# Prompt band attention with the values as matmul weights, two heads in the two column halves of the array

## The chip, the cores and the metric

The kernel runs on one core of a Trainium2 chip. The metric is the device time of one execution in microseconds (us); the median of several runs is reported. Each run of the kernel before is listed below; the profile is that of one further execution.

## What is computed

One step of a one-layer encoder on a prompt of 2048 frames and a sample of 8 x 16 frames: a mixer (band attention beside a convolution), a cross-attention into 256 memory tokens, and a squared-ReLU MLP. The change is in the band attention of the prompt, which has 8 heads of width 64; a frame of chunk c (64 frames) sees the frames of chunks c-8 to c:

```python
s = jnp.einsum('bnqhd,bnkhd->bnhqk', qc, kb).astype(jnp.float32) * (Dh ** -0.5)
s = s + rel_bias(table, q_off, k_off).astype(jnp.float32)[None, None]
s = jnp.where(key_valid[None, :, None, None, :], s, NEG_INF)
p = jax.nn.softmax(s, axis=-1).astype(v.dtype)
o = jnp.einsum('bnhqk,bnkhd->bnqhd', p, vb)
```

## The kernel before, in words

The mixer works through four sets q of four 128-frame tiles (`QT`, line 187; the sample is a fifth tile of set 0). For each set it computes the projections q, k, v and the two GLU halves, writes Q, K and V to scratch in HBM, and runs the convolution as 31 taps on VectorE over four channel blocks (line 451, held in order by a token). The attention of set q runs while set q+1 is projected; that of the last set runs beside the output projection.

The attention of a set (`attn`, line 609) goes head by head, and within a head over its four query tiles i. `attn_load` brings in the head's Q, K, V and bias (lines 537 to 544; K is the tile `ak`, which has two buffers, V is `av`). `scores` multiplies in TensorE (line 564), adds the bias and finds the minimum on VectorE (line 568), and takes the exponential on ScalarE, which also sums it (line 571). `xpose` turns the up to five 128 x 128 blocks of probabilities on TensorE (line 585) and copies them out of PSUM on ScalarE (line 587). `values` multiplies each turned block as the weights (128 columns) with 64 columns of V (line 597) and adds up to five blocks in PSUM (tile `oc`, one buffer). After the fourth tile VectorE takes the reciprocal of the sums (line 602) and scales the result into `a` (line 604); every second head the pair is written to `catd` (line 607). The tiles 0 to 3 of set 0 have 1, 2, 3 and 4 blocks, all the others five: 70 blocks a head, 560 for eight heads.

All pieces are put in one list by times written out by hand (`Plan`, `PAR`, `pl.add(..., attn(q))`, lines 818 to 825); within a stretch the functions of `attn` are spread evenly. That list gives the priority. A scheduler then fixes the order on each engine ahead of the run: of the instructions whose inputs and buffers it reckons ready, the first in the list. So the pieces of one function can be parted by others, and each engine executes its own queue in the order so fixed. Loads of the attention go through SP's queue with those of the weights. All operands of line 597 are F32; the large products of line 122 and the scores are F32R.

Of the kernel before, what the change touches and what calls it, by code (L numbers as in the profile page):

```python
# [11 lines left out]
F32 = mybir.dt.float32  # L12
F32R = mybir.dt.float32r
BF16 = mybir.dt.bfloat16
AF = mybir.ActivationFunctionType
ALU = mybir.AluOpType
# [57 lines left out]
class Kern:  # L74
# [93 lines left out]
    def mixer(self):  # L168
# [4 lines left out]
        with ExitStack() as st:  # L173
# [42 lines left out]
            def bias_tables():  # L216
                anti = mp.tile([P, P], F32, tag="t512", name="anti")
                nc.gpsimd.memset(anti, 0.0)
                nc.gpsimd.affine_select(out=anti, in_=anti, compare_op=ALU.not_equal, fill=1.0,
                                        base=-(P - 1), pattern=[[1, P]], channel_multiplier=1)  # L220
                tab = mp.tile([H, 257], F32, tag="att", name="tab")
                nc.sync.dma_start(tab, I["att_rel_bias"][0])
                ext = mp.tile([H, 768], F32, tag="ak", name="ext")
                nc.vector.tensor_copy(ext[:, 0:256], tab[:, 1:257])
                nc.vector.tensor_copy(ext[:, 256:768], tab[:, 256:257].to_broadcast([H, 512]))
                nc.sync.dma_start(extd, ext)
                far = mp.tile([P, H], F32, tag="far", name="far", bufs=1)
                nc.sync.dma_start(far, view(I["att_rel_bias"], 256, [[0, P], [257, H]]))
                z = mp.tile([P, 384], F32, tag="apr", name="zero")
                nc.gpsimd.memset(z, 0.0)  # L230
                for h in range(H):
                    hk = mp.tile([P, 2, P], F32, tag="av", name="hk")
                    for m in range(2):
                        nc.sync.dma_start(hk[:, m, :], view(extd, h * 768 + m * P, [[1, P], [1, P]]))
                    pt = ps.tile([P, 512], F32, tag="tp", name="pt", bufs=TPB)
                    for m in range(2):
                        nc.tensor.matmul(pt[:, (1 - m) * P:(2 - m) * P], hk[:, m, :], anti, start=True, stop=True)
                    bt = mp.tile([P, 640], F32, tag="ab", name="bt")
                    nc.vector.tensor_scalar(bt[:, 0:384], z, far[:, h:h + 1], -1.0, op0=ALU.add, op1=ALU.mult)
                    nc.vector.tensor_scalar(bt[:, 384:640], pt[:, 0:256], -1.0, None, op0=ALU.mult)  # L240
                    nc.gpsimd.memset(bt[64:128, 0:64], BIG)
                    nc.gpsimd.memset(bt[0:64, 576:640], BIG)
                    nc.sync.dma_start(biasd[h], bt)
                hs = mp.tile([P, 2, P], F32, tag="av", name="hs")
                nc.sync.dma_start(hs[:, 0, :].rearrange("p (h q) -> p h q", h=H), view(extd, P, [[1, P], [768, H], [1, 16]]))
                nc.sync.dma_start(hs[:16, 1, :].rearrange("p (h q) -> p h q", h=H), view(extd, 112, [[1, 16], [768, H], [1, 16]]))
                pt = ps.tile([P, 512], F32, tag="tp", name="pt", bufs=TPB)
                nc.tensor.matmul(pt[:, 0:P], hs[:, 0, :], anti, start=True, stop=True)
                nc.tensor.matmul(pt[:, P:P + 16], hs[:16, 1, :], anti[:16, P - 16:], start=True, stop=True)
                nc.vector.tensor_scalar(sbias[:, 0:P], pt[:, 0:P], -1.0, None, op0=ALU.mult)  # L250
                nc.gpsimd.memset(sbias[:, P:480], BIG)
                nc.vector.tensor_scalar(sbias[:, 240:256], pt[:, P:P + 16], -1.0, None, op0=ALU.mult)
# [273 lines left out]
                return fns  # L526


            A, KQ, PEND, READY = {}, {}, [], []

            def attn_load(q, h):
                def fn():
                    t0 = QT[q][0]
                    k0 = max(0, t0 - 4)
                    nk = t0 + 4 - k0
                    qt = mp.tile([P, 512], F32R, tag="aq", name="aq")
                    nc.sync.dma_start(fr(qt), Qd[h].rearrange("a d t -> (a d) t")[:, t0 * P:t0 * P + 512])
                    kt = mp.tile([P, 2, 1024], F32R, tag="ak", name="ak")
                    for j in range(2):
                        nc.sync.dma_start(fr(kt)[j * HD:(j + 1) * HD, :, :nk * P], Kd[h, :, :, k0 * P:(k0 + nk) * P].rearrange("a d t -> d a t"))  # L540
                    vt = mp.tile([P, 8, HD], F32, tag="av", name="av")
                    nc.sync.dma_start(vt[:, :nk, :], Vd[k0 * P:(k0 + nk) * P, h].rearrange("(j p) d -> p j d", p=P))
                    bt = mp.tile([P, 640], F32, tag="ab", name="ab")
                    nc.sync.dma_start(bt, biasd[h])
                    ss = mp.tile([P, 4], F32, tag="ass", name="ass")
                    KQ[q, h] = (qt, kt, vt, bt, ss, k0)
                return fn

            def scores(q, h, i):
                def fn():  # L550
# [17 lines left out]
                    nc.vector.tensor_tensor_reduce(v3(tt[:, :n]), sp[:, :nb, :w], v3(bt[:, 640 - n:]), op0=ALU.add, op1=ALU.min,  # L568
                                                   scale=1.0, scalar=3e38, accum_out=mn)
                    pr = mp.tile([P, 640], F32, tag="apr", name="apr")  # L570
                    nc.scalar.activation(pr[:, :n], tt[:, :n], AF.Exp, bias=mn, scale=-1.0, accum_out=ss[:, i:i + 1])
                    PEND.append((q, h, i, pr, n, j0 - k0))
                return fn

# [2 lines left out]
            def xpose():  # L577
                q, h, i, pr, n, jo = PEND.pop(0)
                nj = n // P
                pt = mp.tile([P, 5, P], F32, tag="apt", name="apt")  # L580
                for a, b in ((0, min(nj, 3)), (3, nj)):
                    if a < b:
                        tp = ps.tile([P, 512], F32, tag="tp", name="tpa", bufs=TPB)[:, :(b - a) * P]
                        for j in range(a, b):
                            nc.tensor.transpose(tp[:, (j - a) * P:(j - a + 1) * P], pr[:, j * P:(j + 1) * P], self.ident)
                        dst, src = pt[:, a:b, :], tp.rearrange("p (j q) -> p j q", j=b - a)
                        nc.scalar.activation(dst, src, AF.Copy)
                READY.append((q, h, i, pt, nj, jo))

            def values():  # L590
                q, h, i, pt, nj, jo = READY.pop(0)
                qt, kt, vt, bt, ss, k0 = KQ[q, h]
                if i == 0:
                    OC[q, h] = ps.tile([P, 4, HD], F32, tag="oc", name="oc")
                oc = OC[q, h]
                for j in range(nj):
                    nc.tensor.matmul(oc[:, i, :], pt[:, j, :], vt[:, jo + j, :], start=j == 0, stop=j == nj - 1)
                if i == 3:
                    if h % 2 == 0:
                        A[q] = mp.tile([P, 4, P], F32, tag="a", name="a")  # L600
                    r = mp.tile([P, 4], F32, tag="ar", name="ar")
                    nc.vector.reciprocal(r, ss)
                    c = (h % 2) * HD
                    nc.vector.tensor_tensor(A[q][:, :, c:c + HD], oc, r.unsqueeze(2).to_broadcast([P, 4, HD]), op=ALU.mult)
                    if h % 2:
                        t0 = QT[q][0]
                        nc.sync.dma_start(catd[t0 * P:(t0 + 4) * P, (h - 1) * HD:(h + 1) * HD].rearrange("(i p) c -> p i c", p=P), A[q])

            def attn(q):
                fns = [attn_load(q, 0)]  # L610
                for n in range(4 * H + 2):
                    h, i = n // 4, n % 4
                    if n < 4 * H:
                        fns.append(scores(q, h, i))
                    if 0 < n <= 4 * H:
                        fns.append(xpose)
                    if n > 1:
                        fns.append(values)
                    if i == 2 and h + 1 < H:
                        fns.append(attn_load(q, h + 1))  # L620
                return fns


# [7 lines left out]
            def sattn_load(b):  # L631
                def fn():
# [3 lines left out]
                    cv = mp.tile([P, DA], F32, tag="sv", name="scv")  # L636
                    nc.sync.dma_start(cv, I["cache_attn_v"][0, b].rearrange("t h d -> t (h d)"))
                    K = mp.tile([P, 4, 2, 256], F32R, tag="ak", name="sk")
                    Q = mp.tile([P, 4, 2, P], F32R, tag="sqb", name="sq")
                    qs = mp.tile([P, 4, 2, 16], F32, tag="a", name="qs")  # L640

                    nc.gpsimd.memset(fr(Q), 0.0)
# [35 lines left out]
            def sattn_values(b):  # L678
                def fn():
                    V, pr = SA.pop(b)  # L680
                    tp = ps.tile([P, 512], F32, tag="tp", name="tps", bufs=TPB)
                    for s in range(2):
                        nc.tensor.transpose(tp[:, s * P:(s + 1) * P], pr[:, s * P:(s + 1) * P], self.ident)
                    PT = mp.tile([P, 2, P], F32, tag="apt", name="spt")
                    nc.scalar.activation(PT.rearrange("p s c -> p (s c)"), tp[:, :256], AF.Copy)
                    ov = ps.tile([P, 4, 32], F32, tag="oc", name="ov")
                    for p in range(4):
# [726 lines left out]
```

## Time and profile before

| | us |
|---|---|
| runs of the kernel before | 3266.02, 3258.2, 3266.6 (median 3266.02) |
| the profiled execution | 3256.27 |
| its span | 3254.5 |
| TensorE busy | 3129.9 (96%) |
| TensorE weight loads busy | 2679.6 (82%) |
| VectorE busy | 1827.2 (56%) |
| ScalarE busy | 1234.0 (38%) |

A busy time is a sum over instructions that may overlap on the pipelined TensorE; how long a run of matmuls takes is better read from where it begins to where the next one begins. Every F32 matmul leaves two records of a weight load and two of a matmul: line 597 issues 560 and shows 1120. The prompt attention lies between 318 and 1010 us: set 0 from 318, set 1 from 454, set 2 from 692, set 3 from 857 us. The last convolution tap ends at 827 us, the output projection begins after 880 us.

### The profile page before, as it was taken

How to read it: one execution, taken by the hardware profiler on the slowest of the kernel's cores; microseconds unless marked ns; L12 is line 12 of the kernel's file. 1: busy time of each engine (PE TensorE's matmuls, PEld its weight loads, DVE VectorE, ACT ScalarE, POOL GpSimd, SP SyncE). 2: the span in 40 equal slices, each digit the busy share in tenths (PEclk: the TensorE clock that was granted, in tenths of full speed). 3: DMA queues.
4: the chain of work that ended last, by engine and by line, in shares of the span. 5: the costliest groups of instructions: out<-in, count | busy, mean ns of one | idle time of the engine just before them, and what ended most of it. 6: DMA issues, size and time to landing. Idle time of an engine off the chain costs nothing. (4 is left out here: it accounts for less than half of the span.)

```text
span 3254.5 us, 44695 instructions
## 1 busy us (share of the span) xinstructions
PE 3129.9 (96%) x16664; PEld 2679.6 (82%) x16664; DVE 1827.2 (56%) x2812; ACT 1234.0 (38%) x2499; POOL 614.6 (19%) x704
## 2 busy tenths in 40 slices
PE   8889999999899999999999999999999999999998
PEld 7787788979898768788888999988888888888887
DVE  6798979788634435433335444455445544465444
ACT  3223454534554435422224232333334333343332
POOL 4346253342313320022221000002000200020000
PEclk9999999999899999999999999999999999999999
DMA  5465766747864565322224222234233432243222
GB/s 188 122 175 159 210 171 166 195 122 193 241 176 160 189 202 180 102 65 66 64 86 148 81 75 81 75 107 151 93 104 118 145 104 95 91 142 123 91 94 75
DMA packets 309352, 425.18 MB, mean 131 GB/s; under 512 B 62984, under 2 KB 177680, under 8 KB 309062
## 3 DMA queue, kind: packets, MB, share of 16 engines
q1 hardware_dynamic: 300574, 391.38, 40.5%
q0 software_dynamic: 8560, 30.94, 2.4%
q8 instruction: 131, 2.15, 0.3%
q14 instruction: 87, 0.71, 0.1%
HBM read 356.60 MB, written 69.52 MB: 131 GB/s over the span
## 5 line engine op out<-in xcount | busy, mean ns | idle before, releaser
L122 PE MATMUL pu<-xT,wu 128*128 128x512 f32 (+1 forms) x3840 | 756.3, 358 | 3.2 <-DVE xT L95 2.5
L122 PE MATMUL pd<-wd,h 128*128 128x512 f32 x3264 | 750.6, 390 | 1.4 <-DVE y L1336 1.1
L122 PEld LDWEIGHTS pu<-xT,wu 128*128 128x128 f32 x3840 | 659.9, 188 | 95.8 <-DVE xT L95 2.7
L122 PEld LDWEIGHTS pd<-wd,h 128*128 128x128 f32 x3264 | 611.3, 188 | 129.8 <-DVE y L1336 1.5
L122 PE MATMUL pm<-xT,w 128*128 128x512 f32 (+3 forms) x1992 | 423.2, 363 | 11.8 <-POOL w L95 6.2
L451 DVE SCALAR_TENSOR_TENSOR acc<-u,wdT,acc 128x512 f32<-128x512 f32 x480 | 429.7, 895 | 6.4
L103 POOL TENSOR_SCALAR nm<-nss 128x1 f32<-128x1 f32 x103 | 29.7, 288 | 2025.8 <-ACT nsq L132 1078.6
L122 PEld LDWEIGHTS pm<-xT,w 128*128 128x128 f32 x1992 | 337.6, 194 | 52.0 <-POOL w L95 6.5
L94 ACT ACTIVATE wd<-wst 128x512 fp32r<-128x512 f32 x256 | 159.8, 631 | 430.9 <-PE pd L122 364.5
L95 POOL TENSOR_TENSOR w<-wst,w 128x512 fp32r<-128x512 f32 x154 | 229.1, 1502 | 319.9 <-ACT w L94 296.2
L1336 DVE TENSOR_TENSOR y<-pd,y 128x512 f32<-128x512 f32 x238 | 163.5, 688 | 205.0 <-PE pd L122 204.9
L1318 DVE SCALAR_TENSOR_TENSOR hh<-pu,r 128x512 f32<-128x512 f32 (+1 forms) x160 | 96.8, 609 | 321.1 <-ACT r L1317 320.9
L1317 ACT ACTIVATE r<-pu 128x512 f32<-128x512 f32 (+1 forms) x160 | 83.8, 528 | 364.6 <-PE pu L122 356.5
L95 DVE TENSOR_TENSOR wu<-wst,wu 128x512 fp32r<-128x512 f32 x256 | 170.9, 690 | 86.7 <-ACT wu L94 85.7
L95 DVE TENSOR_TENSOR wd<-wst,wd 128x512 fp32r<-128x512 f32 x256 | 182.1, 735 | 35.7 <-ACT wd L94 35.1
L122 PE MATMUL pm<-wo,cT 128*128 128x512 f32 x816 | 200.4, 398 | 0.0
L94 ACT ACTIVATE wu<-wst 128x512 fp32r<-128x512 f32 x256 | 157.7, 630 | 100.6 <-DMA wst<-w_ffn_up 69.2
L122 PE MATMUL y<-mo,pT 128*128 128x512 f32 x768 | 187.1, 398 | 0.0
L122 PE MATMUL sc<-m,xT 128*128 128x512 f32 x768 | 182.0, 392 | 0.3 <-ACT xT L94 0.2
L122 PEld LDWEIGHTS pm<-wo,cT 128*128 128x128 f32 x816 | 151.3, 189 | 33.6 <-issue 2.9
L122 PEld LDWEIGHTS y<-mo,pT 128*128 128x128 f32 x768 | 142.9, 188 | 33.2
L122 PEld LDWEIGHTS sc<-m,xT 128*128 128x128 f32 x768 | 142.9, 188 | 30.8 <-DVE xT L95 0.5
(246 smaller groups left out, 3677.0 us busy)
## 6 DMA issues: line engine op xcount, KB each, us to landing
wst<-w_ffn_up SPq DMA_DIRECT2D x256, 256.0 KB, 3.2
wst<-w_ffn_down SPq DMA_DIRECT2D x256, 256.0 KB, 3.1
wst<-w_in SPq DMA_DIRECT2D x160, 256.0 KB, 3.9
ak<-Kd SPq DMA_DIRECT2D x48, 512.0 KB, 6.8
ab<-biasd SPq DMA_DIRECT2D x32, 320.0 KB, 4.2
cx<-catd SPq DMA_DIRECT2D x17, 512.0 KB, 7.4
x1d<-oy POOLq DMA_DIRECT2D x17, 512.0 KB, 5.9
nx<-x1d SPq DMA_DIRECT2D x17, 512.0 KB, 4.1
```

Of the source, the lines that this page charges most:

```text
L94: nc.scalar.activation(hi, src, AF.Copy)
L95: return (lo_eng or nc.vector).tensor_sub(lo, src, fr(hi))
L103: nc.gpsimd.tensor_scalar(m, ss, 1.0 / count, EPS, op0=ALU.mult, op1=ALU.add)
L122: self.nc.tensor.matmul(out, lhs(a), rhs(b), start=first and n == 0, stop=last and n == 2)
L451: i = nc.vector.scalar_tensor_tensor(o, s, wdT[:, c, w:w + 1], o, op0=ALU.mult, op1=ALU.add)
L1317: nc.scalar.activation(r, pm, AF.Relu)
L1318: nc.vector.scalar_tensor_tensor(hh, pm, 0.0, r, op0=ALU.max, op1=ALU.mult)
L1336: nc.vector.tensor_add(y, pm, y)
```

## The change

`values` now takes V as the weights (64 columns) and the turned probabilities as the moving operand (128 columns). It does this for the two heads of a pair together: head 2g writes PSUM partitions 0 to 63 from the left half of the array's columns, head 2g+1 partitions 64 to 127 from the right half (`tile_position`), block by block in turn. The result stands transposed (channel by query); once per pair ScalarE copies it to SBUF (`ot`), and a new `heads_out` turns it back with four TensorE transposes and scales both heads at once. The four tiles of the two heads are taken in the order `ORDER`, so that both heads' loads are live at the same time; `av` gets three buffers, `apt` four, and the sample attention's `sq` moves to the tag `qkv`. The load of head h+2 stands behind the last scores of head h.

```diff
+            def values(q, g, i):
+                def fn():
+                    if i == 0:
+                        OC[q, g] = ps.tile([P, 4, P], F32, tag="oc", name="oc")
+                    oc = OC[q, g]
+                    hs = [READY.pop((q, 2 * g + x, i)) + (KQ[q, 2 * g + x][2],) for x in range(2)]
+                    nj = hs[0][1]
+                    for j in range(nj):
+                        for x, (pt, _, jo, vt) in enumerate(hs):
+                            nc.tensor.matmul(oc[x * HD:(x + 1) * HD, i, :], vt[:, jo + j, :], pt[:, j, :], start=j == 0, stop=j == nj - 1,
+                                             tile_position=(0, x * HD))
+                    if i == 3:
+                        ot = mp.tile([P, 4, P], F32, tag="t512", name="ot")
+                        nc.scalar.activation(ot, oc, AF.Copy)
+                        OC[q, g] = ot
+                return fn
+            def heads_out(q, g):
+                def fn():
+                    ot, ss = OC.pop((q, g)), SUM.pop((q, g))
+                    tp = ps.tile([P, 512], F32, tag="tp", name="tpv", bufs=TPB)
+                    for i in range(4):
+                        nc.tensor.transpose(tp[:, i * P:(i + 1) * P], ot[:, i, :], self.ident)
+                    r = mp.tile([P, 4, 2], F32, tag="ar", name="ar")
                     nc.vector.reciprocal(r, ss)
+                    A = mp.tile([P, 4, P], F32, tag="a", name="a")
+                    nc.vector.tensor_tensor(A.rearrange("p i (x d) -> p (i x) d", x=2), tp.rearrange("p (n d) -> p n d", d=HD),
+                                            r.rearrange("p i x -> p (i x)").unsqueeze(2).to_broadcast([P, 8, HD]), op=ALU.mult)
...
+            ORDER = ((0, 0), (0, 1), (1, 0), (0, 2), (1, 1), (0, 3), (1, 2), (1, 3))
             def attn(q):
+                steps = [(2 * g + x, i) for g in range(H // 2) for x, i in ORDER]
+                fns = [attn_load(q, 0), attn_load(q, 1)]
+                for n in range(len(steps) + 3):
+                    if n < len(steps):
+                        fns.append(scores(q, *steps[n]))
+                    if 0 < n <= len(steps):
+                        fns.append(xpose)
+                    if 1 < n < len(steps) + 2:
+                        h, i = steps[n - 2]
+                        if h % 2:
+                            fns.append(values(q, h // 2, i))
+                    if n > 2:
+                        h, i = steps[n - 3]
+                        if h % 2 and i == 3:
+                            fns.append(heads_out(q, h // 2))
+                    if n < len(steps):
+                        h, i = steps[n]
+                        if i == 3 and h + 2 < H:
+                            fns.append(attn_load(q, h + 2))
                 return fns
```

## Rows read from the trace of the kernel before

**Rows 1.** Page, first part: busy us, share of the span, instructions of each engine.

```profile
PE 3129.9 (96%) x16664; PEld 2679.6 (82%) x16664; DVE 1827.2 (56%) x2812; ACT 1234.0 (38%) x2499; POOL 614.6 (19%) x704
```

**Rows 2.** Busy time by stretch: the attention of sets 0, 1, 2 and 3.

```profile
318.00:454.00 136.00, 122.33 (x767) 107.84 (x766) 118.99 (x202) 64.27 (x168) 44.64 (x37) 0.94 0.71 197
454.00:692.00 238.00, 219.01 (x1375) 195.04 (x1375) 199.54 (x276) 111.17 (x241) 106.70 (x85) 0.98 0.63 168
692.00:857.00 165.00, 159.62 (x1087) 146.42 (x1087) 135.29 (x216) 81.37 (x184) 44.84 (x35) 0.98 0.69 187
857.00:1010.00 153.00, 144.71 (x917) 130.87 (x917) 66.79 (x125) 86.39 (x204) 33.33 (x45) 0.94 0.63 178
```

**Rows 3.** Waits from 300 to 1010 us: sum, times, longest.

```profile
DVE att L568 <- PE sc L564: 59.2, 29, 10.0
PE sc L564 <- DVE amn L568: 24.2, 13, 7.2
```

**Rows 4.** Groups of matmuls by line: busy us, mean ns, idle before.

```profile
L597 PE MATMUL oc<-av,apt 128*128 128x64 f32 x1120 | 146.0, 274 | 11.0 <-ACT apt L587 6.9 <-DVE a L604 3.9
```

**Rows 5.** Timeline of weight loads in set 2: start, us, engine, line, count.

```profile
710.33 0.61 PEld L585 LDWEIGHTS tpa<-ident,apr 128*128 128x128 f32 x5
710.91 1.20 PEld L597 LDWEIGHTS oc<-av,apt 128*128 128x128 f32 x10
712.03 0.53 PEld L122 LDWEIGHTS pm<-xT,w 128*128 128x128 f32 x3
```

**Rows 6.** Timeline of matmuls in the sample's cross-attention, four column groups.

```profile
1185.19 1.07 PE L965 MATMUL so<-sv,spT 128*32 128x256 f32 x16
```

**Rows 7.** Timeline of weight loads around the same place.

```profile
1184.44 0.59 PEld L916 LDWEIGHTS pt<-ident,sk 128*128 128x128 f32 x4
1185.19 0.59 PEld L965 LDWEIGHTS so<-sv,spT 128*32 128x32 f32 x16 [0.17 <-issue]
1186.19 0.85 PEld L916 LDWEIGHTS pt<-ident,sk 128*128 128x128 f32 x8 [0.41 <-issue]
```

**Rows 8.** Line 965 by itself: duration of one in ns, min/median/max.

```profile
L965 PE MATMUL so<-sv,spT x128: 379/379/403, 1117.7 to 1234.5; 128*32 128x256 f32 x128
```

**Rows 9.** Timeline of matmuls: first and last value groups parted as 6 and 4.

```profile
801.24 0.88 PE L597 MATMUL oc<-av,apt 128*128 128x64 f32 x6
...
802.60 0.55 PE L597 MATMUL oc<-av,apt 128*128 128x64 f32 x4
...
1003.99 0.78 PE L597 MATMUL oc<-av,apt 128*128 128x64 f32 x6
...
1005.67 0.56 PE L597 MATMUL oc<-av,apt 128*128 128x64 f32 x4
```

**Rows 10.** Groups of VectorE and ScalarE instructions, 300 to 1010 us.

```profile
L604 DVE TENSOR_TENSOR a<-oc,ar 128x256 f32<-128x256 f32 x32 | 13.4, 418 | 16.9 <-PE oc L597 16.9
L95 DVE TENSOR_TENSOR xT<-pt,xT 128x512 fp32r<-128x512 f32 x16 | 10.4, 682 | 6.4 <-ACT xT L94 6.4
L602 DVE RECIPROCAL ar<-ass 128x4 f32<-128x4 f32 x32 | 5.5, 171 | 3.6 <-ACT apr L571 3.5
...
L366 ACT ACTIVATE ko<-pt 128x512 f32<-128x512 f32 x4 | 2.4, 597 | 7.2 <-issue 3.9 <-PE pt L364 3.4
```

**Rows 11.** SP's timeline: the two K loads of head 3, set 2.

```profile
726.01 0.65 SPq L540 DMA_DIRECT2D ak<-Kd  x1
...
734.26 0.60 SPq L540 DMA_DIRECT2D ak<-Kd  x1
```

**Rows 12.** ScalarE's timeline: first exponential of head 2 and of head 3.

```profile
733.77 0.84 ACT L571 ACTIVATE apr<-att,amn 128x640 f32<-128x640 f32 x1
...
755.64 0.84 ACT L571 ACTIVATE apr<-att,amn 128x640 f32<-128x640 f32 x1
```

**Rows 13.** Page, DMA issues: count, KB each, median us to landing.

```profile
ak<-Kd SPq DMA_DIRECT2D x48, 512.0 KB, 6.8
```

More of the change, by code (lines that the diff above doesn't have):

```diff
@@ L231, in bias_tables @@
                 for h in range(H):
-                    hk = mp.tile([P, 2, P], F32, tag="av", name="hk")
+                    hk = mp.tile([P, 2, P], F32, tag="av", name="hk", bufs=3)
                     for m in range(2):
@@ L243, in bias_tables @@
                     nc.sync.dma_start(biasd[h], bt)
-                hs = mp.tile([P, 2, P], F32, tag="av", name="hs")
+                hs = mp.tile([P, 2, P], F32, tag="av", name="hs", bufs=3)
                 nc.sync.dma_start(hs[:, 0, :].rearrange("p (h q) -> p h q", h=H), view(extd, P, [[1, P], [768, H], [1, 16]]))
@@ L526, in lns @@
                 return fns
-            A, KQ, PEND, READY = {}, {}, [], []
+            KQ, SUM, PEND, READY = {}, {}, [], {}
             def attn_load(q, h):
@@ L540, in fn @@
                         nc.sync.dma_start(fr(kt)[j * HD:(j + 1) * HD, :, :nk * P], Kd[h, :, :, k0 * P:(k0 + nk) * P].rearrange("a d t -> d a t"))
-                    vt = mp.tile([P, 8, HD], F32, tag="av", name="av")
+                    vt = mp.tile([P, 8, HD], F32, tag="av", name="av", bufs=3)
                     nc.sync.dma_start(vt[:, :nk, :], Vd[k0 * P:(k0 + nk) * P, h].rearrange("(j p) d -> p j d", p=P))
@@ L544, in fn @@
                     nc.sync.dma_start(bt, biasd[h])
-                    ss = mp.tile([P, 4], F32, tag="ass", name="ass")
-                    KQ[q, h] = (qt, kt, vt, bt, ss, k0)
+                    if h % 2 == 0:
+                        SUM[q, h // 2] = mp.tile([P, 4, 2], F32, tag="ass", name="ass")
+                    KQ[q, h] = (qt, kt, vt, bt, SUM[q, h // 2], k0)
                 return fn
@@ L570, in fn @@
                     pr = mp.tile([P, 640], F32, tag="apr", name="apr")
-                    nc.scalar.activation(pr[:, :n], tt[:, :n], AF.Exp, bias=mn, scale=-1.0, accum_out=ss[:, i:i + 1])
+                    nc.scalar.activation(pr[:, :n], tt[:, :n], AF.Exp, bias=mn, scale=-1.0, accum_out=ss[:, i, h % 2:h % 2 + 1])
                     PEND.append((q, h, i, pr, n, j0 - k0))
@@ L579, in xpose @@
                 nj = n // P
-                pt = mp.tile([P, 5, P], F32, tag="apt", name="apt")
+                pt = mp.tile([P, 5, P], F32, tag="apt", name="apt", bufs=4)
                 for a, b in ((0, min(nj, 3)), (3, nj)):
@@ L587, in xpose @@
                         nc.scalar.activation(dst, src, AF.Copy)
[L588 to L601, printed above, removed]
-                    nc.vector.reciprocal(r, ss)
[L603 to L607, printed above, removed]
@@ L609, in attn @@
-            def attn(q):
[L610 to L615, printed above, removed]
-                        fns.append(xpose)
[L617 to L620, printed above, removed]
+                READY[q, h, i] = pt, nj, jo
@@ new lines, in heads_out @@
+            def heads_out(q, g):
[5 more added lines that the diff above has]
+                    r = mp.tile([P, 4, 2], F32, tag="ar", name="ar")
+                    nc.vector.reciprocal(r, ss)
+                    A = mp.tile([P, 4, P], F32, tag="a", name="a")
+                    nc.vector.tensor_tensor(A.rearrange("p i (x d) -> p (i x) d", x=2), tp.rearrange("p (n d) -> p n d", d=HD),
+                                            r.rearrange("p i x -> p (i x)").unsqueeze(2).to_broadcast([P, 8, HD]), op=ALU.mult)
+                    t0 = QT[q][0]
+                    nc.sync.dma_start(catd[t0 * P:(t0 + 4) * P, g * P:(g + 1) * P].rearrange("(i p) c -> p i c", p=P), A)
+                return fn
@@ L638, in fn @@
                     K = mp.tile([P, 4, 2, 256], F32R, tag="ak", name="sk")
-                    Q = mp.tile([P, 4, 2, P], F32R, tag="sqb", name="sq")
+                    Q = mp.tile([P, 4, 2, P], F32R, tag="qkv", name="sq")
                     qs = mp.tile([P, 4, 2, 16], F32, tag="a", name="qs")
@@ L683, in fn @@
                         nc.tensor.transpose(tp[:, s * P:(s + 1) * P], pr[:, s * P:(s + 1) * P], self.ident)
-                    PT = mp.tile([P, 2, P], F32, tag="apt", name="spt")
+                    PT = mp.tile([P, 2, P], F32, tag="apt", name="spt", bufs=4)
                     nc.scalar.activation(PT.rearrange("p s c -> p (s c)"), tp[:, :256], AF.Copy)
```

## The prediction, made before the changed kernel ran

> **What bounds the kernel now.** I read the page's busy line first, then the busy time by stretch, the waits, and the timelines of TensorE. TensorE is busy 96% of the span, the next engine 56% [rows 1]; the time is TensorE's queue, and a change is worth what it takes out of that queue where nothing else is full. The change lies wholly in the attention of the prompt, so the four stretches count [rows 2]. In that of set 0 TensorE is busy 122.33 of 136 us and VectorE 118.99; in set 1 219.01 and 199.54 of 238: there the two are nearly level. In set 2 TensorE has 159.62 of 165 us, VectorE 135.29; in set 3 TensorE 144.71 of 153, VectorE 66.79. Between them the two wait on each other: VectorE waited 59.2 us for scores, TensorE 24.2 us for VectorE to empty the scores [rows 3].
>
> **The values themselves.** Line 597 left 1120 records for its 560 matmuls [rows 4]. In a whole group of five blocks, ten records, the first weight load stands at 710.91 and the next line's at 712.03: 1.12 us, 0.112 a record [rows 5]. Streaming 64 columns twice as fast would not help there, since each record brings its own load of 128 columns. All of them: 1120 x 0.112 = 125.4 us, 8.96 us for two heads of one set with four full tiles, 4.48 for set 0 (10 blocks a head).
>
> After the change there are again 560 matmuls and 1120 records, with 64 columns of weights and 128 of moving data, in two column halves. The trace has such halves as quarters: line 965 runs four column groups with 256 moving columns. Its 16 records span 1.07 us [rows 6] though each lasts at least 0.379 [rows 8], so the last begins some 0.69 us after the first; four rounds of four lie in that, three steps of about 0.215 us once 0.05 is taken off for the first load and the stagger. The groups do overlap. Half the columns: 0.11 us for a round of two records, or 560 x 0.11 = 61.6 us in 560 rounds. If the time of a round did not depend on the columns it would be 0.215 and the sum 120.4; if the columns passed only once it would be 0.055 and 30.8 us. I take 0.11, since twice 256 columns in 0.215 us is 2.4 GHz, and leave the ends to the range. Gain: 125.4 - 61.6 = 63.8 us.
>
> **What each excursion into the halves costs.** The weight loads before line 965 end at 1185.03 (1184.44 + 0.59) [rows 7]; loads in a row overlap by some 0.03, so the next was due at 1185.00 and came at 1185.19: 0.19 us. From its first load to the first load after it 1.00 us pass, 0.14 more than four rounds of 0.215. A load of 64 columns is longer than one of 32 by about 0.03. Together 0.36 us for each time that TensorE enters and leaves the halves, and it does so at least once for each of 4 pairs x 16 tiles, 64 times.
>
> The Trainium skill, "TensorEngine Tiling (Array Packing)", section Performance Considerations, offers up to twice the speed for swapping the operands and tiling the columns where 64 are needed; by that alone the gain would be some 63 us, and the 0.36 us of these rows takes over a third of it back.
>
> More often where the scheduler parts a group: from set 1 on I found ten value groups cut into 6 and 4 records, nine of them after 857 us, the first and the last shown [rows 9]. So of the 16 groups in set 3 I let five or six be cut: 6 more excursions, 2.2 us. There the first head's two blocks run alone, since their inputs are ready two steps earlier and the scheduler takes what is ready: 4 rounds x 0.11 x 5 = 2.2 us of lost overlap. Excursions 64 x 0.36 = 23.0 us.
>
> **Transposes.** Four for each of 16 pairs and sets, 64. Five in a row take 0.61 us as weight loads [rows 5], less than 0.12 each; I take 0.11: 7.0 us. They are neighbours of other transposes or matmuls of the full array and need no excursion.
>
> **Sum on TensorE.** Set 0: 4 x (4.48 - 2.2 - 1.44) - 1.75 = 1.6 us. Sets 1 and 2: 4 x (8.96 - 4.4 - 1.44) - 1.75 = 10.7 each. Set 3: 10.7 - 2.2 - 2.2 = 6.3. Together 29.3 us.
>
> **What passes to the end.** Set 0: VectorE fills 87% of the stretch, nothing. Set 1: TensorE idles 19 us already, I let half pass, 5.4. Set 2: TensorE 97% busy, VectorE has 30 us left, 80%, 8.6. Set 3: the output projection fills every gap and VectorE is half idle, 80%, 5.0. That is 19 us; the ends are 0 and 29.
>
> **The other engines.** VectorE loses 32 reciprocals (5.5 us) and 32 scalings (13.4 us) and gets 16 of each; a 128x512 operation from PSUM takes 682 ns, a reciprocal 171 [rows 10]: 13.6 us, a saving of 5 us that is already in the shares above. ScalarE gets 16 copies of 128x512 at 597 ns [rows 10], 9.6 us, in stretches where it is busy 64 of 136 to 86 of 153 us [rows 2]. They lie beside TensorE's work: the one `oc` is wanted again only three steps later (some 5 us each, 165 us over 32 steps). If that cover failed, each of 16 would cost TensorE at most its 0.6 us.
>
> **Loads.** K has two buffers, and both heads of a pair now hold one. Before, the two K loads of head 3 in set 2 left at 726.01 and 734.26 [rows 11], ahead of head 2's first exponential at 733.77 or level with it, and head 3 began its own at 755.64 [rows 12]: over 20 us of lead. After the change a K buffer comes free with the sixth of a pair's eight steps and its successor is due at the ninth, 10 to 15 us later, while two loads 8 us apart with 6.8 us to landing [rows 13] need 15. SP waits at that load for line 564, and behind it stand the weight loads of the projections. Other TensorE work covers most of a late load, so between nothing and 1.5 us each for 24 heads, 36 us, I take 3. The loads of V gain a buffer, which works the other way. The sample's `sq`, moved to another tag, overlaps the projection's `e` only at its end; I put it at nothing.
>
> **Sum.** 3256.3 - 19 + 3 = 3240 us against the profiled execution's 3256.27. The median of the runs shown is 3266.02, 9.8 more, the lowest 3258.2; so I expect a median of 3250.
>
> **Rivals.**
> - VectorE holds the pace. For it: sets 0 and 1 nearly level [rows 2], 24.2 us of waits for it [rows 3]. Against: in sets 2 and 3 it has room. Then only set 3 pays, 5 us less the 3 for loads: 3264.
> - The weight load isn't hidden in the halves. The Trainium skill, "TensorE: Matmul & The Clock Gate", section Part 3: Packing small matmuls, says loads overlap running matmuls only when the row group differs; both halves have the same rows. As a mechanism here: a 64-column load, half of 0.112, stands ahead of each of 560 rounds, 31 us, and the change is worth 2 us the wrong way, 3268. Against it: line 965's groups share their rows too, and its rounds leave no room for a load [rows 6].
> - The two heads don't meet (the slower side). The first head's probabilities are ready two steps early. If the scheduler issues that head's blocks as soon as they are ready, all 1120 records run one at a time, 1120 x 0.11 = 123 us, and 64 x 0.36 + 7 = 30 us come on top of a gain of 2: 28 us, 80% of it on the path, 3288; apart in two excursions each, 23 more. It decides from the point where more than half of the groups are parted. Against it: nearly all groups of sets 1 and 2 stood whole [rows 5].
> - The loads are late as in the upper bound: -19 + 36 = +17, 3283. For it the arithmetic above, against it the other work that TensorE has at hand.
>
> **Chances.** The forecast 0.58 (3235 to 3262), VectorE 0.19, the unhidden load 0.05, the parted heads 0.08, the late loads 0.10. Above the range lies half of the parted and late cases; below it the case in which all 29 us and some of the waits go, 3230. Range 3228 to 3282. A difference under 0.3%, about 10 us, can't be told from none. Of the forecast 0.50 is faster by more than that and 0.08 is not; VectorE gives 0.07 faster and 0.12 same; the unhidden load is same; the late loads 0.05 same, 0.05 slower; the parted heads slower. Faster 0.57, same 0.30, slower 0.13.
>
> **What would show it.** Line 597's successor should show 1120 records of 128x128 moving columns on 64, in pairs that begin within a few hundredths of a us, rounds of 0.11, a whole group of five within about 1.46 us. About 70 gaps of 0.2 us in the weight loads. Values below 90 us altogether, 64 new transposes, 16 copies of 600 ns. The stretches of sets 2 and 3 should be shorter, set 0 not. Wrong if the halves' records follow one another at 0.11, if there are many more than 80 excursions, if scores wait for K, or if the time saved comes back as TensorE waiting for line 568.

## The result, and the profile after

Four runs each on one chip: 3303.76 us (3302.12 to 3307.55) after the change, 3262.11 us (3257.62 to 3266.6) before it, a ratio of 1.0124 with an interval of 1.0108 to 1.0141. The change costs 41.7 us where a gain was forecast. The profiled executions, 3307.55 and 3256.27 us, lie 51 us apart. Among the runs below, one of f2's ten took 6686.75 us: it counts in f2's median (3277.99 without it) but not in its ratio.

The busy line of the profile's page, against [rows 1]:

```profile
PE 3141.7 (95%) x16728; PEld 2644.2 (80%) x16728; DVE 1813.8 (55%) x2780; ACT 1243.7 (38%) x2515; POOL 608.7 (18%) x704
```

TensorE is still nearly always busy, and the kernel is longer: this line alone can't say why. The attention of sets 0 to 3 by stretch, against [rows 2] (after the span and its length: busy us and count of PE, PEld, DVE, ACT, POOL, then granted clock, DMA share, GB/s; the cuts of [rows 2] are moved by the lag of the instructions around them; set 2's first step alone runs at 696 us, 40 us ahead of its second, and falls into set 1's stretch):

```profile
347.00:483.00 136.00, 125.92 (x783) 102.61 (x783) 117.17 (x195) 67.02 (x174) 45.37 (x38) 0.92 0.71 195
483.00:733.00 250.00, 225.84 (x1418) 191.43 (x1419) 197.58 (x265) 113.41 (x246) 105.31 (x85) 0.94 0.60 160
733.00:907.00 174.00, 151.03 (x1078) 128.19 (x1077) 136.22 (x210) 84.51 (x189) 44.76 (x37) 0.94 0.68 180
907.00:1064.00 157.00, 140.52 (x926) 111.72 (x926) 61.90 (x113) 85.73 (x203) 30.94 (x43) 0.93 0.58 167
```

Three things are to be seen. The first stretch begins at 347 us instead of 318: most of the loss has come before the changed product first runs. Sets 1, 2 and 3 take 250, 174 and 157 us instead of 238, 165 and 153, though TensorE is busy for a smaller share of them (set 2: 87% against 97%). And the granted clock is lower, 0.94 in sets 1 and 2 against 0.98.

The product's own rows do show the saving (groups of instructions: busy us, mean ns, idle before):

```profile
L601 PE MATMUL oc<-apt,av 128*64 128x128 f32 x1120 | 90.9, 284 | 10.8 <-ACT apt L588 8.5 <-DMA av<-Vd 2.3
L614 PE MATMUL tpv<-ident,ot 128*128 128x128 f32 x64 | 11.2, 296 | 4.8 <-ACT ot L605 4.8
L605 ACT ACTIVATE ot<-oc 128x512 f32<-128x512 f32 x16 | 9.5, 591 | 8.7 <-PE oc L601 8.6
L618 DVE TENSOR_TENSOR a<-tpv,ar 128x512 f32<-128x512 f32 x16 | 11.0, 687 | 9.9 <-PE tpv L614 9.8
```

and the timeline of weight loads around one whole group, against [rows 5]:

```profile
772.90 0.72 PEld L565 LDWEIGHTS sc<-ak,aq 128*128 128x128 f32 x4
773.81 1.07 PEld L601 LDWEIGHTS oc<-apt,av 128*64 128x64 f32 x20 [0.19 <-issue]
775.05 0.30 PEld L122 LDWEIGHTS pm<-xT,w 128*128 128x128 f32 x2 [0.17 <-issue]
```

Ten rounds, 20 records for two heads, take 775.05 - 773.81 = 1.24 us up to the next load, and 0.19 us of idle stand ahead; before, the two heads took 2 x 1.12 us. Of the 32 runs of 20 records, 30 take this 1.24. The waits of the attention (345 to 1060 us; sum, times, longest), against [rows 3]:

```profile
DVE att L569 <- PE sc L565: 51.7, 24, 10.7
PE sc L565 <- DVE amn L569: 37.8, 23, 3.6
```

TensorE's wait for VectorE to empty the scores has grown from 24.2 to 37.8 us.

### The profile page after: what moved, and what is told of

It is laid out like the page before. It is cut to its first block, busy times and chain, and to the rows that moved or that the text cites. A ratio compares the mean times of both kernels' runs of the same rounds, so it can differ in the third digit from the quotient of the medians.

```text
span 3305.7 us, 44767 instructions
## 1 busy us (share of the span) xinstructions
PE 3141.7 (95%) x16728; PEld 2644.2 (80%) x16728; DVE 1813.8 (55%) x2780; ACT 1243.7 (38%) x2515; POOL 608.7 (18%) x704
## 5 line engine op out<-in xcount | busy, mean ns | idle before, releaser
L122 PE MATMUL pm<-xT,w 128*128 128x512 f32 (+3 forms) x1992 | 434.5, 370 | 13.9 <-DVE e L95 3.1
L122 PEld LDWEIGHTS pm<-xT,w 128*128 128x128 f32 x1992 | 345.2, 198 | 61.2 <-POOL w L95 4.9
```

The source lines that it names most:

```text
L122: self.nc.tensor.matmul(out, lhs(a), rhs(b), start=first and n == 0, stop=last and n == 2)
```

## The experiments

"The kernel before" gave 3263.6, 3264.24, 3262.83, 3262.99 and 3264.79 us beside the five sets of runs below. All times are medians.

**Which part costs: tag, buffers, product, order.** e1 is the kernel before with the tag of `sq` alone changed; e2 the changed kernel with `sq` on buffers of its own.

```diff
e1: -Q = mp.tile(..., tag="sqb", name="sq")    +Q = mp.tile(..., tag="qkv", name="sq")
e2: -Q = mp.tile(..., tag="qkv", name="sq")    +Q = mp.tile(..., tag="sqb", name="sq")
    (room: scv moved to tag "ab", svn and saT to "aq")
```

> The kernel before with one edit: the sample attention's tile sq takes its two buffers from the tag qkv, which the projection's e uses, and no longer has its own. Theory A (the tag): this edit alone makes the sample attention start and end some 20 us later, so 3262 + 20 to 30 = 3282 to 3292, with the first sq memset no longer before 20 us and the prompt attention beginning near 345 instead of 318 us. Rival B (the new product or order of the prompt attention shifts the schedule as a whole): within 8 us of 3262, the prompt attention still at about 318.

> The changed kernel, but sq has two buffers of its own again; room for them comes from the sample's cached V moving to the tag ab and two small sample tiles to aq, which nothing else uses in that stretch. Theory A: the sample attention is back to its old pace, 3304 - 25 = about 3279, still slower than before by some 16 us that belong to the prompt attention. Rival B: unchanged, 3300 or more.

e1: 3259.4 us, ratio 0.9988 (0.9976 to 1.0001). e2: 3300.9 us, 1.0111 (1.0089 to 1.0133). The tag is not it, alone or undone.

e3 keeps the changed order, loads and buffers and goes back to the old product, without copy and turning; e4 runs a step's two heads one after the other instead of by turns.

```diff
e3: +nc.tensor.matmul(oc[:, i, x * HD:(x + 1) * HD], pt[:, j, :], vt[:, jo + j, :], ...)
e4: -for j in range(nj): for x, ... in enumerate(hs):
    +for x, ... in enumerate(hs): for j in range(nj):
```

> The changed kernel with the old product: probabilities as weights, 64 columns of V moving, no column halves, no copy by ScalarE, no turning back; the order of the two heads, the loads, the buffers and sq's tag stay as changed, and one scaling a pair. Theory A, with a new product that is worth what TensorE's records say (about 100 us against 149 from first load to next load, less entries and 64 transposes): slower than the changed kernel by 10 to 25 us, 3314 to 3329. Rival C (the new product loses what it saves by its copy, turning and waits): 3285 to 3304.

> The changed kernel with the two loops of the product swapped: all blocks of the first head, then all of the second, so the halves of the array don't work at the same time. If TensorE sets the pace of the prompt attention, the some 60 us of overlap lost pass mostly to the time: 3335 to 3355. If VectorE holds the pace there (a rival of the prediction), at most 10 us more: 3304 to 3314.

e3: 3302.86 us, 1.0118 (1.0103 to 1.0133), the same as the changed kernel. So the product is not what costs, and it gains nothing that can be told from none (0.9 us); the loss lies in the rest. e4: 3315.04 us, 1.0155 (1.0139 to 1.0171). Its whole group in the timeline of weight loads:

```profile
785.17 1.78 PEld L601 LDWEIGHTS oc<-apt,av 128*64 128x64 f32 x20 [0.36 <-issue]
787.12 0.59 PEld L565 LDWEIGHTS sc<-ak,aq 128*128 128x128 f32 x4 [0.17 <-issue]
```

1.95 us instead of 1.24: the interleaving does its work. From the first load of each run of values to the next line's load, all runs together take 132.6 us instead of 100.5, and the kernel is 11 us longer. So about a third of what is added reaches the end; what is taken away, it turns out below, doesn't.

**The third buffer of the values.** b1 is the kernel before with three buffers under the tag `av`, as in the change, for all who use it (and `sq` on "qkv"). Those are the attention's values and two tiles of the bias tables, `hk` and `hs`, in the first 200 us. f1 is the changed kernel with these two on another tag; f2 does the same to e3; f3 is the kernel before with all the change's buffers, and `hk`, `hs` off `av`.

```diff
b1: -tag="av", name="hk")  +tag="av", name="hk", bufs=3)   (hs and av alike)
f1: -tag="av", name="hk", bufs=3)  +tag="aq", name="hk")    (hs alike)
```

> The kernel before with sq on the tag qkv (which alone changed nothing) and three buffers for the tag av, that of the bias tables' hk and hs as well. Everything else, the prompt attention too, as before. Theory A2: the third buffer lets the scheduler run the bias tables ahead and place the sample attention's transposes and scores later in TensorE's queue (62 products of line 122 more ahead of the first); the sample attention starts some 20 us late and most of it stays: 3264 + 20 to 30 = 3284 to 3294. Rival B2 (the slip in the sample attention comes back later, the loss is that of the prompt attention's order): within 10 us of 3264.

> The changed kernel with hk and hs on the tag aq (two buffers, free at that time) instead of av, so that the sample attention's place in the queue is that of the kernel before; all else as changed. Theory A2: 3304 - 20 to 30 = 3274 to 3284. Rival B2: 3295 to 3305.

> The order of the two heads with the old product (as in the run of the order alone), with hk and hs on the tag aq. Beside the run of the changed kernel with the same edit it prices the new product where the sample attention isn't late. If the product is worth its TensorE time it is 10 to 25 us slower than that run; if the lateness of both was the same and the product is worth nothing, the two are equal within 4 us, at 3275 to 3285.

> The kernel before with all the changed buffers (av three in the prompt attention, apt four, sq on qkv) but hk and hs on aq; old order and old product. Theory A2: the same as before within 6 us, 3258 to 3270, so that what the run with hk on its own tag is slower than this is the new order of the heads. Rival: the third V buffer of the prompt attention itself costs, 3275 or more.

b1: 3289.13 us, 1.007 (1.0047 to 1.0093). f1: 3276.71 us, 1.0031 (1.0017 to 1.0045). f2: 3278.41 us, 1.0039 (1.0027 to 1.0051). f3: 3265.13 us, 1.0005 (0.9991 to 1.002). A third buffer for the bias tables costs 25 us alone and gives 27 back when it is undone. How can a buffer more make a kernel slower? The order of each engine's queue is laid down ahead of the run. With three buffers, more of the tables' loads and stores go ahead of the sample attention. SP's timeline, the changed kernel and then f1 (`hk` a load for the tables, `sck` the sample's first keys):

```profile
190.84 2.08 SPq L234 DMA_DIRECT2D hk<-extd  x4
...
201.52 0.32 SPq L243 DMA_DIRECT2D biasd<-bt  x1
...
216.77 0.43 SPq L661 DMA_DIRECT2D sck<-cache_attn_k  x1
```

```profile
174.42 0.42 SPq L661 DMA_DIRECT2D sck<-cache_attn_k  x1
...
192.32 0.80 SPq L234 DMA_DIRECT2D hk<-extd  x2
```

The sample's keys are asked for at 217 instead of 174 us. On TensorE 1094 matmul records of the projections (line 122) stand ahead of the first transpose of `sck` instead of 1032, counted in the traces: 1094 in the changed kernel and in b1, 1032 before and in f1. The sample's first exponential comes at 244.28 us (changed kernel) and 245.98 (b1) against 223.86 before and 225.16 in f1, and the first 20 us of delay are never made up.

The loss splits into the steps of this series, each the difference of two neighbours: 27.1 (third buffer, changed kernel against f1), -1.7 (product, f1 against f2), 13.3 (order of the heads, f2 against f3), 0.9 (other buffers, f3 against before) and 2.1 between the two medians of before, in all 41.7 us. Two of them stand on a second pair as well: the buffer on b1 (25 us), the product on e3 (0.9 us). The order's 13 us include its loads, which bring in both heads of a pair together. What is left to explain is why the order costs 13 us and the product gives 2.

**Keys, or VectorE?** h1 is f1 with a third key buffer, taken by heads 2 and 5; its room comes from moving `scv`, `svn` and `saT` as in e2. t1, t2 and t3 are f1, f2 and f3 with 16 of the convolution's 31 taps.

```diff
h1: +kt = mp.tile(..., tag="ak3" if h % 3 == 2 else "ak", bufs=1 if h % 3 == 2 else 2)
t*: -[tap(w) for w in range(1, 31)]   +[tap(w) for w in range(1, 16)]
```

> The changed kernel with the bias tables off the attention values' buffers (as f1_hk_own_tag, 3276.7 us) and with a third buffer for the band's keys, taken in turn (two, two, third), its room won by giving three small tiles of the sample attention other buffers. Theory K: the 13 us that the new order of the heads costs are key loads that wait, because the order holds both key buffers until a pair's last step; then the gaps at the change of set (18.3 us from set 2 to set 3 in f1_hk_own_tag, 8.2 before) shrink to under 12 and the time falls by 8 to 14, to 3263 to 3269. Rival O: the order costs through what stands behind what on VectorE and TensorE, and the keys are hidden; then 3274 to 3280.

> f1_hk_own_tag with 16 of the 31 taps of the depthwise convolution (240 VectorE instructions of about 0.9 us each left out, some 215 us of its 1814). Theory V: the product's saving of TensorE (41 us of weight loads and values, 16 net) isn't passed on because VectorE sets the pace of the attention; with the taps gone this kernel lies 10 to 18 us under t2_short_conv_order_only. Rival D: the saving is lost in the deal between TensorE and its buffers whatever VectorE does; then the two stay within 4 us, as f1 and f2 are.

> f2_order_only_hk (old product, new order of the heads) with 16 of the 31 taps. Theory V: the order's 13 us too are VectorE's (conv instructions ahead of the scores that the order needs); then it lies within 4 us of t3_short_conv_before. Theory K (key loads that wait): still 9 to 15 us above t3.

> f3_buffers_old_attention (old product, old order, new buffers but for the bias tables; 3265.1 us) with 16 of the 31 taps: the base of t1 and t2. If VectorE sets the pace of the attention it falls below f3 by more than the 7.4 us of idle TensorE between 300 and 692 us: 15 to 60 us; if VectorE is hidden, under 10 us.

h1: 3273.28 us, 1.0033 (1.002 to 1.0045), 3.4 under f1, which neither theory had, and by the ratios no difference from it. At the change of set, heads 6 and 7 and the next set's 0 and 1 still share two buffers in h1 (from the start of set 2's last exponential to that of set 3's first 15.4 us pass, 18.3 in f1), so h1 prices the third buffer inside a set and not there.

t1, t2, t3: 3240.19, 3240.02 and 3228.15 us. Without 15 taps, some 215 us of VectorE, each of the three gains 36 to 38 us. VectorE is therefore part of what sets the pace, but theory V falls: product and order stand as they did, +0.2 us and +11.9. The stretch from 300 to 1060 us of t3, t2 and t1 (busy us and count of PE, PEld, DVE, ACT, POOL, clock, DMA share, GB/s):

```profile
300.00:1060.00 760.00, 727.85 (x4590) 649.49 (x4590) 429.27 (x709) 381.93 (x877) 255.09 (x241) 0.97 0.67 186
```

```profile
300.00:1060.00 760.00, 716.82 (x4537) 635.84 (x4537) 417.09 (x666) 374.19 (x862) 250.01 (x232) 0.98 0.67 185
```

```profile
300.00:1060.00 760.00, 707.12 (x4587) 588.44 (x4586) 412.66 (x665) 382.84 (x878) 245.88 (x231) 0.96 0.67 185
```

VectorE is busy 54 to 56% of it, and still the new product (third line against the second) turns 10 us of TensorE's work into idle time. The granted clock of the stretch is lower too, 0.975 in t2 and 0.962 in t1 before rounding, which is 760 x 0.0135 = 10 us of full speed; each is one execution.

**The start of set 3.** In the profiles f2 falls behind f3 most of all in one place: at set 2's last exponential it lies 6 us back (856.5 against 850.1 us), at set 3's first 22 (880.3 against 858.5), at the end of the span 16. There TensorE's waits (850 to 892 us) and SP's timeline of f2 are

```profile
PE sc L565 <- DVE amn L569: 12.9, 3, 9.6
PE sc L565 <- DMA ak<-Kd: 5.8, 1, 5.8
```

```profile
850.96 0.68 SPq L537 DMA_DIRECT2D aq<-Qd  x1
851.68 0.58 SPq L540 DMA_DIRECT2D ak<-Kd  x1
...
858.02 0.91 SPq L540 DMA_DIRECT2D ak<-Kd  x1
```

and the same loads of set 3's first head in the kernel before:

```profile
828.16 0.38 SPq L537 DMA_DIRECT2D aq<-Qd  x1
828.59 0.58 SPq L540 DMA_DIRECT2D ak<-Kd  x1
...
833.99 0.58 SPq L540 DMA_DIRECT2D ak<-Kd  x1
```

The set's first keys leave 23 us later. By the program the last pair of set 2 holds both key buffers to its end; that this alone delays the loads isn't shown, since SP also waited 16.1 us for VectorE's `lnd` between 820 and 885 us. The keys meet the loads of the output weights, eight of 512 KB, whose splits (`wo`) stand ahead of the softmax (`att`) on ScalarE and VectorE and wait for them, which makes the 9.6 us. ScalarE's and VectorE's timelines of f2:

```profile
874.86 1.06 ACT L94 ACTIVATE wo<-wos 128x1024 fp32r<-128x1024 f32 x1 [7.36 <-DMA wos<-w_out]
```

```profile
875.95 1.22 DVE L95 TENSOR_TENSOR wo<-wos,wo 128x1024 fp32r<-128x1024 f32 x1 [7.66 <-ACT wo L94]
877.10 0.69 DVE L505 TENSOR_TENSOR lnd<-lnd,lnr 128x512 f32<-128x512 f32 x1
877.70 0.82 DVE L569 CUSTOM_DVE_ANT_0 att<-sc,ab 128x640 f32<-128x640 f32 x1
```

w1, w2 and w3 are f1, f2 and f3 with one of the eight weights loaded and split and used for all.

```diff
 def load_wo(k):
+    if k: OP["w"].append(OP["w"][0]); return
```

p1 takes the other half apart: the changed product in the order and loads of before, with `hk` and `hs` off `av` as in f1, and `scv`, `svn` and `saT` moved as in e2 for room. Both heads' values are taken in the second head's steps, so p1 and f3 differ in a little more than the product.

```diff
-ORDER = ((0, 0), (0, 1), (1, 0), (0, 2), (1, 1), (0, 3), (1, 2), (1, 3))
+ORDER = [(x, i) for x in range(2) for i in range(4)]
-tag="apt", name="apt", bufs=4)    +tag="apt", name="apt", bufs=6)   (and the loads as before)
```

> f1_hk_own_tag (new product, new order; 3276.7 us) with one of the eight pieces of the output weights loaded and split, and used for all eight. Theory L: the order's 13 us arise at the start of set 3, where the two heads' loads (both at the set's start, and later than before) and the output weights' 4 MB share the DMA engines while the weights' splits stand ahead of the softmax on ScalarE and VectorE; without the weights this kernel falls by 12 to 20 us more than w3 does from f3, to within 4 us of w3 or below it. Rival K: the keys' buffers alone; then it stays 8 to 13 us above w3.

> f2_order_only_hk (old product, new order; 3278.4 us) with one of the eight pieces of the output weights. Theory L: within 4 us of w3. Rival K: 8 to 13 us above it. If the product's saving is lost at the same stalls, w1 lies 6 or more us under this kernel.

> f3_buffers_old_attention (old product and order; 3265.1 us) with one of the eight pieces of the output weights: the base of w1 and w2. It should fall by the 5 to 10 us that TensorE sits idle between 849 and 905 us, to 3255 to 3262.

> The changed product (values as weights in column halves, turned back once per pair) with the order of the heads and the loads of the kernel before: head 0's four blocks, then head 1's, whose value steps do both heads; six buffers for transposed probabilities instead of four, paid for by giving three small tiles of the sample attention other buffers; bias tables off the values' buffers. Base: f3_buffers_old_attention, 3265.1 us. Theory S: what the product saves on TensorE is lost at the stalls that the new order makes, most of them at the start of set 3, so without that order it shows: 3248 to 3257. Rival W: the product's saving turns into waits on VectorE and ScalarE wherever it stands; then 3261 to 3268, and with the value steps bunched in the second head perhaps more.

w1, w2, w3: 3263.35, 3267.06 and 3251.46 us. All fall by 11 to 14, so the weights cost every version about the same, and the order still costs 15.6 us (w2 against w3). Theory L falls. Its rival named the keys; with the weights gone the gap into set 3 in the profiles is 12.9 us in w2 against 8.3 in w3, which covers 5 of the 15.6 and leaves 11 without a place.

p1: 3265.95 us, 1.0013 (1.0003 to 1.0023). Without the new order the loss of 42 us is down to 3, so order and tables' buffer were all of it; and the product is still worth nothing (f3: 1.0005). Theory S falls, W holds. The stretch from 300 to 1060 us of f3 and TensorE's longest waits in it, then the same of p1:

```profile
300.00:1060.00 760.00, 707.68 (x4414) 631.23 (x4413) 553.29 (x864) 369.12 (x848) 254.27 (x229) 0.95 0.65 179
```

```profile
PE sc L564 <- DVE amn L568: 24.9, 16, 7.1
PE oc L597 <- ACT apt L587: 8.4, 5, 4.3
```

```profile
300.00:1060.00 760.00, 684.74 (x4475) 570.31 (x4474) 553.75 (x836) 372.27 (x855) 257.94 (x232) 0.95 0.66 180
```

```profile
PE sc L565 <- DVE amn L569: 42.5, 27, 7.1
PE tpa L586 <- ACT apr L572: 9.1, 11, 2.4
```

TensorE works 23 us less in the same time (p1 enters this stretch and leaves it some 4 us behind f3), and waits 18 us more for the scores' buffer and about 8 more for exponentials. The clock isn't where the saving goes: it is 0.95 in both. There is one buffer for scores: step n + 1 can't begin before VectorE has read step n. From the last score matmul of a step to the end of VectorE's part 1.9 us (f3) and 2.0 us (p1) pass on average. TensorE's other work between two steps is shorter than that step's own handoff in 20 of the 127 pairs of steps in f3 and in 37 in p1.

**A second score buffer.** x0 is f3, x1 is p1 with two buffers for scores; the projections' matmul groups, which had two banks, share three with the transposes, and the accumulators of `kvp`, after the attention, move to the scores' buffers.

```diff
-tag="sc", name="sc")           +tag="sc", name="sc", bufs=2)
-tag="mm", name="pm", bufs=2)   +tag="tp", name="pm", bufs=TPB)
```

> f3_buffers_old_attention (old product and order, 3265.1 us) with a second PSUM buffer for the prompt's scores. Its two banks come from the matmul groups of the projections, which now take turns with the transposes in three banks instead of having two of their own. In f3 TensorE stands idle 45 us between the scores of one step and of the next, in 20 of 126 steps because the work between them is shorter than VectorE's part of the handoff. Theory H (the single score buffer is the pace): those waits shrink to under 15 us and the time falls by 5 to 20 us, to 3245 to 3260. Rival D: the three shared banks cost as much or more, 3265 to 3290.

> p1_product_old_order (new product, old order, 3266.0 us) with the same second buffer for scores. There the idle time between scores is 71 us, and 37 of 126 steps have too little work between. Theory H: the product's 25 us on TensorE weren't passed on because each step waited for VectorE to empty the only score buffer; with two it shows, and this kernel lies 8 to 20 us under x0_two_score_buffers_before. Rival E: the wait moves to the next handoff (exponentials, transposes); then within 4 us of x0.

x0: 3326.46 us, 1.0181 (1.0163 to 1.0198). x1: 3323.87 us, 1.018 (1.0166 to 1.0194). Theory H falls in both. Rival E holds; D is right in sign, though its range ended at 3290. The exchange of banks costs 61 and 58 us, of which 34 (x0 against f3) and 41 (x1 against p1) have come by the prompt's first exponential, before the second buffer can serve the prompt. So whether a second buffer for scores would pay by itself isn't shown; only x0 and x1 can be compared. From 340 to 1100 us TensorE's waits in x0 and then x1 are:

```profile
PE sc L564 <- DVE amn L568: 10.6, 7, 3.9
PE tpa L585 <- ACT apr L571: 8.1, 6, 4.1
PE oc L597 <- ACT apt L587: 7.7, 4, 5.6
```

```profile
PE sc L565 <- DVE amn L569: 16.3, 16, 3.8
PE tpa L586 <- ACT apr L572: 14.3, 11, 2.9
PE tpa L586 <- ACT apt L588: 11.1, 7, 5.7
```

The wait for the score buffer shrinks, and with the new product TensorE waits longer at the next two handoffs, exponentials and copies of transposed probabilities; the product is worth 2.6 us, no clear gain. Of the kernels that do the whole work none beats the kernel before; e1 and f3 are level with it, p1 lies 3 us behind.

## Why the prediction was wrong

The measured 3303.76 us lie 53.8 above the forecast of 3250 and outside its range. Of these the tables' buffer, which had no term, makes 27.1, the order of the heads 13.3 - 3 = 10.3, and the saving that didn't pass to the end 19 - 1.7 = 17.3; other buffers and the two medians of before make 3.0, and 3.9 go the other way, since the median of before fell to 3262.11 with its fourth run. Two of the prediction's signs of being wrong came true: 99 excursions, and time that comes back as TensorE waiting for VectorE to empty the scores.

**The halves: right.** Records in pairs within 30 ns (501 of the 1021 neighbours within a run), rounds near 0.11 us, and ahead of the first load an idle time of 0.12 to 0.25 us in 83 of 99 runs (median of all 99 0.17; the 0.19 given counts a usual overlap of loads, 0.03, on top of such an idle time); the group shown takes 1.24 + 0.19 = 1.43 us with its entry, where at most 1.46 was given. The weight load is hidden, so that rival falls. The Trainium skill, "TensorE: Matmul & The Clock Gate", section Part 3: Packing small matmuls — row/col tiling, says in its list of what overlaps that loads run beside matmuls only where the row group differs. Both halves use all the rows here, and 20 loads and 20 matmuls fit into 1.24 us, so this trace disagrees with that line.

**Excursions: too few.** 99 and not 70, above all because 28 pieces of one block of one head (two records) ran by themselves. One such piece and the rest of its group in the changed kernel's timeline of weight loads:

```profile
543.05 0.19 PEld L601 LDWEIGHTS oc<-apt,av 128*64 128x64 f32 x2 [0.16 <-issue]
543.41 0.19 PEld L122 LDWEIGHTS pm<-xT,w 128*128 128x128 f32 x1 [0.17 <-issue]
543.83 1.06 PEld L601 LDWEIGHTS oc<-apt,av 128*64 128x64 f32 x18 [0.24 <-ACT apt L588]
```

The first block runs ahead, and the other head's probabilities come later. Most of these pieces take 0.36 us from their load to the next line's (21 of 28). From the first load of a run to the next line's load the values took 149.0 us before and 100.5 after (waits inside runs counted). Less 99 x 0.19 for the entries and 64 x 0.11 for the transposes, both at the prediction's sizes, that leaves an estimate of 23 us net where the sum had 29.3. A small miss.

**"What passes to the end": the failed step for the product.** 19 us were to pass on and -1 to 4 did: f1 against f2 1.7, t1 against t2 -0.2, w1 against w2 3.7, x1 against x0 2.6, p1 against f3 -0.8. I read the high busy share of sets 1 and 2 [rows 2] as room on the other engines. It is an average. What counts, as far as these runs tell, is whether TensorE has work between two steps of one chain (scores, minimum on VectorE, exponential on ScalarE, transposes, copy, values) in a queue whose order is fixed; the queue had been filled for the long values, and shorter ones leave a gap: between f3 and p1 the short pairs go from 20 to 37 and the wait for the scores' buffer from 24.9 to 42.5 us. The wait of 24.2 us in [rows 3] was the sign of it, and I used it for one rival only. That rival, VectorE holding the pace, gave 3264, close to p1, but not for its reason: halving the taps did not let the gain through.

**The tables' buffer: no term at all.** The diff showed `bufs=3` for `hk` and `hs`, 150 us ahead of the attention, and the prediction says of the buffers only that the loads of V gain one, "which works the other way". This was 27 of the 41.7 us, and it came at the sample attention, which the prediction doesn't look at but for `sq`.

**The order of the heads: sized too small.** "Between nothing and 1.5 us each ..., I take 3" became 13. The place was partly as foretold (set 3's first keys leave late), but the cost did not come in small late loads; in f2's profile most of it came at one change of set.

**What stays open.** No single resource was found that holds the 13 us of the order: a third key buffer inside a set gave at most 3, the output weights 0, VectorE's taps 1. A third buffer for queries, keys and biases across the change of set would tell; no run has it. Nor is it shown which handoff sets the pace once the product is short. x0 and x1 show the wait growing at the next handoff when one is relieved, in kernels that other banks had slowed by 60 us.

## What to carry to other kernels

A busy share of 97% on TensorE does not mean that a us taken from it is a us gained: look first at the shortest cover between two dependent steps in its queue, and count the steps where it is already too short. A buffer count is an edit like any other: where the queues' order is laid down ahead, one more buffer can move unrelated loads in front of urgent ones, so list every user of the tag and find its place in the queue. Price a change's three parts (arithmetic, order, buffers) apart, each with a kernel of its own; here the part that the change was about was the smallest.

## What the runs showed of the hardware

Two column halves that share all rows run as pairs with their weight loads hidden: 0.124 us a round over a whole group in the changed kernel. There TensorE's loads stand idle for 0.17 us (median of 99 runs) ahead of the halves, and a run of two records takes 0.36 us from its load to the next line's. Taking the halves one after the other costs 1.95 us for the same 20 records (e4). In the changed kernel sets 1 and 2 idle more than before and were granted less clock, 0.94 against 0.98, means over a clock that stands at 2.4 or at 1.2 GHz. The two don't always go together: from 300 to 1060 us p1 idles 23 us more than f3, and both were granted 0.95.
